# Expert gate and up weights loaded in runs of 2 KB, with the token rows stored in permuted channel order

## The chip, the cores and the metric

The program runs on one core of a Trainium2 chip. Its five engines work side by side: TensorE (PE, matrix products), VectorE (DVE), ScalarE (ACT), GpSimd (POOL) and SyncE (SP, which issues most of the transfers). Sixteen DMA engines of the core move data between DRAM and the on-chip memory of 128 partitions. The metric is the device time of one execution in microseconds, lower is better.

## The reference, cut to what matters

Two decoder layers over 1024 tokens of 1024 channels. Each layer has four mixers side by side, an output projection, and then a mixture of experts. The last part is what the change touches:

```python
def hier_moe(h, w_rg, b_rg, w_re, b_re, w_gate, w_up, w_down):
    ...
    for e in range(N_EXPERTS):
        he = jax.nn.silu(t @ w_gate[e]) * (t @ w_up[e])
        y = y + comb[:, e:e + 1] * (he @ w_down[e]).astype(f32)
    return y.reshape(B, S, D).astype(h.dtype)
...
x = x + hier_moe(rms_norm(x, ffn_norm[l]), ...)
```

There are 16 experts per layer. `w_gate[e]` and `w_up[e]` are [1024, 256], `w_down[e]` is [256, 1024], all in float32. Each token goes to two experts; `comb` is zero for the others.

## The kernel before

**Mixing stage.** `mix_stream` takes the eight token tiles of 128 tokens in order. `mix_b` multiplies a tile by the output projection, adds the residual (xm), writes it to the accumulator in DRAM (L1505; `xacc` in layer 0, the output in layer 1), and computes the second norm: L1509 is one VectorE instruction over [128 tokens, 1024 channels] that multiplies xm by the inverse root r1 and by the gain, and L1510 writes the result to `hbuf` in DRAM, one row of 4 KB per token. `mix_c` computes the routing logits from xm, not from the normed tile. The stage is interleaved with the last attention tiles.

**Expert stage.** `moe` walks 16 experts. The first two are fixed; the other 14 come by falling token count, a wide tile (256 slots) and a narrow one (128 slots) in turn. For expert e the program's order is: `expert_up(e)`; `expert_in(e+1)`; the weights W(e+1), with their loads and conversions; the gather G(e+2); `expert_down(e)`. The kernel is written against a framework that plans the order in which instructions stand on each engine, allocates the rotating buffers and puts in the waits, so the order on an engine need not be that of the text.

- `gather` (L1799): an indirect transfer, issued by POOL, fetches 128 rows of `hbuf` by slot number into xg; one per narrow expert, two per wide one.
- `expert_in`: PE transposes xg (eight blocks of 128 channels), ACT and DVE write the transposed tile as a rounded part and a remainder, xh[:, k] and xl[:, k], k = 0 to 7. Partition p of block k holds channel 128 k + p of the row as it is stored.
- `expert_weights` (L1741 to L1755): four units u of gate and up, two of down. A unit is a raw tile of [128, 1024] float32 (4 KB per partition). For gate and up, unit u holds the two channel blocks k = 2u and 2u + 1 of both matrices, laid out as (k, t, n): block, matrix (0 gate, 1 up), 256 columns. Each matrix comes with one transfer of 256 KB (L1749), in which each partition has two pieces, rows 256 u + p and 256 u + 128 + p, of 1 KB each. The raw tiles rotate through six places, one expert's worth, so that a load can start when the conversion of the same unit of the expert before is done.
- `split_unit`: each unit is converted in two halves of 512 columns, on ACT (rounded part wh, L165) and on DVE (remainder wl, L173). With the layout (k, t, n) a half is one block k of both matrices.
- `up_wide`, `up_narrow`: products over k and t, three matmuls for each (wh with xh, wh with xl, wl with xh, in either operand order), L177 to L179.
- `expert_down` (L1867): ACT scales the product rows (L1866), and POOL issues an indirect transfer that adds 128 rows of 4 KB to the accumulator in DRAM. Since all of them write the same tensor, they follow one another.

SP issues all loads and plain stores, POOL all gathers and scatter-adds. In the profile, queue q1 carries SP's transfers and q0 POOL's; both run on the same 16 DMA engines.

Of the kernel before, what the change touches and what calls it, by code (L numbers as in the profile page):

```python
# [14 lines left out]
ALU = mybir.AluOpType  # L15
# [3 lines left out]
D = 1024  # L19
# [23 lines left out]
class Region:  # L43
    """Tiles laid out by hand in pages of 8 KB: per page its kind (r: only float32r, f: anything else) and a list of
    (tag, 4-byte columns, copies). A tag with a plus shares its place with the tag after it; a tag may have copies in
    several pages. A page is taken when its first tile is, so that a phase can start while the one before it still
    holds other pages."""
# [35 lines left out]
def both(*gens):  # L83
    """alternates between generators; returns their results"""
    res = [None] * len(gens)
    live = list(range(len(gens)))
    while live:
        for k in list(live):
            try:
                next(gens[k])  # L90
            except StopIteration as e:
                res[k] = e.value
                live.remove(k)
            else:
                yield
    return res


class Trunk:
# [14 lines left out]
    # ---------------------------------------------------------------- tiles  # L114
# [23 lines left out]
    def psum(self, two):  # L138
        """the other four banks: two pairs (two) or four single ones"""
        if self.pq:  # L140
            self.pq[0].close()
        c = ExitStack()
        self.pqn += 1
        self.pq = (c, c.enter_context(self.tc.tile_pool(name=f"pq{self.pqn}", bufs=1, space=PSUM, reuse_waits="tile")), two)
# [9 lines left out]
    # ---------------------------------------------------------------- helpers  # L154
# [3 lines left out]
    def copy(self, out, in_):  # L158
        """a copy on ScalarE, every third on VectorE"""
# [31 lines left out]
    def rsqrt(self, ms, k):  # L191
        """(ms + eps) ** -0.5 for a [P, k] tile of mean squares"""
# [19 lines left out]
    # ---------------------------------------------------------------- constants  # L212
    def constants(self):
# [11 lines left out]
        # -1 on the real half, +1 on the imaginary half  # L225
# [7 lines left out]
    # masks, block scores, routing  # L233
    def constants2(self):
# [19 lines left out]
        # block scores that are forced or lie ahead: [128 q, tile, 16]  # L254
# [11 lines left out]
        # routing: token order, slots, small counters  # L266
# [20 lines left out]
    # reduced sine and cosine of an angle tile, each in [-pi, pi]  # L287
# [21 lines left out]
    # cos and signed sin tables: [128 tok, tile, half pairs], mla 16 pairs then nsa 8 pairs  # L309
# [27 lines left out]
    def rope(self, x, B, half, i, e1, e2):  # L337
        """x [P, B, 2 * half] in place, with row i of the tables, on two engines"""
# [13 lines left out]
    # ---------------------------------------------------------------- layer vectors  # L352
    def layer_vectors(self, l):
# [14 lines left out]
        # queries carry the scale of the scores and a minus  # L368
# [7 lines left out]
        # [128 ch, 2 chunks, ...]  # L376
# [14 lines left out]
        # softplus(-lam) = max(-lam, 0) + log1p(exp(-|lam|)), log1p(e) = 2 atanh(e / (2 + e))  # L391
# [24 lines left out]
        # block-diagonal gate weights [128 in, (gate, chunk), 128 out]  # L416
# [12 lines left out]
    # ---------------------------------------------------------------- input projection  # L429
    def mixer_norm(self, l, src):  # L430
        """pre-norm and its transposed halves hT"""
# [25 lines left out]
    def mixer_in(self, l):  # L457
        """channel-major columns of w_in: yields (first column, half of the tokens, psum)"""
# [14 lines left out]
    def tok_units(self, l, part, V):  # L473
        """token-major columns: c_q c_kv k_pe gate (part 0) or nsa_q k_slc v_slc k_win v_win (part 1)"""
# [18 lines left out]
    def mixer_in_tok(self, us):  # L493
        """yields (token tile, its columns), and None after each quarter of the products"""
# [20 lines left out]
    def mla_weights(self, l, V, pages):  # L515
        """up-projections, split, in the free columns 728.. of the pages, 256 columns at a time"""
# [22 lines left out]
    def prep_nsa(self, l, i, z, V):  # L539
        """queries, keys and values of a token tile, normalised and rotated, to zq"""  # L540
# [18 lines left out]
    def prep_mla(self, l, i, z, V):  # L559
        """queries, keys and values of a token tile, normalised and rotated, to zm; gates to zq"""  # L560
# [47 lines left out]
    # ---------------------------------------------------------------- RG-LRU  # L608
# [47 lines left out]
    # ---------------------------------------------------------------- S5  # L656
    # Chunks of 8 steps: y = K u + C A^(t+1) s, s' = A^8 s + sum A^(7-t) B u, with s kept in a frame that
    # turns with the phase of A^8, so that the recurrence over chunks is real.
    def s5_gen(self, l, wide):
        """tables of a layer; wide: mostly on the vector engine, phases of eight groups at once in raw pages"""  # L660
# [67 lines left out]
        # the sign of the imaginary phases, per half  # L728
# [25 lines left out]
        # input matrix times (A - 1) / a  # L754
# [42 lines left out]
        # powers in falling order  # L797
# [4 lines left out]
        for b in range(4):  # L802
# [27 lines left out]
            # response to a step, lags 7 .. 0, then zeros  # L830
# [20 lines left out]
    # u, psum [128 ch, 512 tok] -> ud [256 ch, 8, 128]  # L851
# [19 lines left out]
    def s5_block(self, l, b, io):  # L871
        """four groups, in three steps"""
# [27 lines left out]
        # rows (t, c'): column s' of row t holds lag 7 - s' - t  # L900
# [25 lines left out]
    def s5_run(self, l):  # L926
        """all blocks, staggered"""
# [47 lines left out]
    # ---------------------------------------------------------------- NSA  # L975
    def nsa_compress_in(self, half, pt):
        """k_cmp | v_cmp channels; each with a copy shifted by one token below or above it"""
# [10 lines left out]
    def nsa_compress(self, l, V):  # L988
        nc, v, I = self.nc, self.nc.vector, self.I
        hid = []  # L990
        for nm, src, o in (("k", self.KC, 0), ("v", self.VC, 1)):
# [5 lines left out]
            # token 16 c + 2 j (+ parity on the second half of the partitions)  # L997
# [57 lines left out]
    def nsa_prep(self, i):  # L1055
        """transposed and split queries and keys of tile i, its compressed blocks and its block choice"""
# [43 lines left out]
    def nsa_cmp(self, q):  # L1100
# [12 lines left out]
        # rows without a block keep their sum at zero  # L1113
# [54 lines left out]
    def merge_out(self, po, heads, P):  # L1168
        """transposed output rows [P, heads * 128], P = 64 channels or 128, their two halves [Vh | Vl]"""
# [4 lines left out]
    def merge(self, ot, y, heads, coef, first, tag, P):  # L1174
        """y [128, heads, 64] (+)= coef [128, heads] * output rows"""
# [14 lines left out]
    def soft(self, S_, k, n, P, acc):  # L1190
        """P = exp(min(S_) - S_) and its row sums, for k rows of n negated scores"""
# [7 lines left out]
    def nsa_scores(self, q, br):  # L1199
        """probabilities of the selected blocks (br 0) or of the window (br 1); two heads at a time where they are short"""  # L1200
# [70 lines left out]
    def nsa_stream(self, tiles):  # L1271
        """the token tiles in order, each next to the preparation of the one after it"""
# [16 lines left out]
    def beside(self, run, side, i):  # L1289
        """steps of run, each with one of the side generator, whose result goes to Qn[i]"""  # L1290
# [102 lines left out]
    def mla_stream(self):  # L1393
        """pairs of token tiles in order, the scores of a head next to the values of the one before"""
# [15 lines left out]
    # ---------------------------------------------------------------- output projection, router  # L1410
    def mix_stream(self, l, src):
        """w_out with the residual, the second norm and the routing logits, pipelined over the token tiles"""
# [29 lines left out]
    def out_weights(self, l):  # L1442
        """w_out times the gains of its inputs, split"""
# [13 lines left out]
    def mix_a(self, i):  # L1457
        """mixer outputs of a token tile, normalised, transposed and split"""
# [17 lines left out]
    def mix_b(self, i, yT):  # L1476
        """projection and residual, then the second norm"""
# [18 lines left out]
        else:  # L1496
            # both halves together, so that the pages of w_out come free early
# [11 lines left out]
        v.scalar_tensor_tensor(xt, xm, r1, mx["fgain"], op0=ALU.mult, op1=ALU.mult)  # L1509
# [3 lines left out]
    def mix_c(self, i, h, r1):  # L1513
        """routing logits"""
# [581 lines left out]
```

## Time and profile before

| | |
|---|---|
| device time, median of 3 runs | 2251.12 us |
| lowest and highest run | 2242.23 and 2265.75 us |
| span of the profiled execution, first to last instruction | 2249.8 us |
| bytes moved by DMA | 301.49 MB in 268,176 packets |
| packets of queue q1 (SP) | 253,592 with 246.82 MB |
| packets of queue q0 (POOL) | 14,400 with 52.44 MB |
| engines' share of the span | PE 84%, DVE 59%, ACT 49%, POOL 27% |

The profile is of one execution, and gives the span alone, not that execution's device time. An engine's busy time is the sum of its instructions; a share over the whole span is a mean over stages with different limits, so the stages are read by windows of time. "Idle before" an instruction is put down to what came last by the profile. A DMA packet is one contiguous run that one DMA engine moves.

### The profile page before, as it was taken

What the parts mean: (1) busy time and instruction counts of PE and PEld (TensorE: products, weight loads), DVE (VectorE), ACT (ScalarE), POOL (GpSimd) and SP (SyncE); (2) the same over time, 40 slices, a digit from 0 to 9 for tenths busy, and PEclk for the clock granted to TensorE, in tenths of its full rate; (3) what the DMA queues carried; (4) which work ended last, traced back from release to release, by engine and by line L of the source; (5) the groups of instructions that cost most, each with busy time, mean ns of one, the idle gap of its engine ahead of it and who ended that gap; (6) DMA issues with size and microseconds to landing.
All of it is one profiled execution on the core that took longest, in us unless ns stands there. A gap on an engine that the chain in (4) does not pass through costs nothing. (4 is left out here: it accounts for less than half of the span.)

```text
span 2249.8 us, 32167 instructions
## 1 busy us (share of the span) xinstructions
PE 1896.9 (84%) x10722; PEld 1491.7 (66%) x10722; DVE 1324.1 (59%) x3167; ACT 1112.7 (49%) x2432; POOL 616.0 (27%) x1007
## 2 busy tenths in 40 slices
PE   4759899999899877867767798999999998788886
PEld 3548876656677766756656578765557776777775
DVE  5966655465565567865534356555665555766663
ACT  4055544455454435544544555445654453465553
POOL 2432542000111136666411215420101111322121
PEclk9879998899999878988988899988998998899998
DMA  7345332022212548867774353320222124598874
GB/s 191 127 109 134 112 119 67 24 57 86 77 62 83 191 122 230 236 203 229 205 185 151 99 125 114 116 68 24 62 91 67 68 88 180 164 267 241 257 215 113
DMA packets 268176, 301.49 MB, mean 134 GB/s; under 512 B 93784, under 2 KB 221656, under 8 KB 267992
## 3 DMA queue, kind: packets, MB, share of 16 engines
q1 hardware_dynamic: 253592, 246.82, 34.9%
q0 software_dynamic: 14400, 52.44, 10.5%
q8 instruction: 89, 1.46, 0.3%
q14 instruction: 95, 0.78, 0.1%
HBM read 215.79 MB, written 78.18 MB: 131 GB/s over the span
## 5 line engine op out<-in xcount | busy, mean ns | idle before, releaser
L173 DVE TENSOR_TENSOR wl<-raw,wh 128x512 fp32r<-128x512 f32 (+3 forms) x294 | 221.1, 778 | 94.6 <-ACT wh L165 87.7
L165 ACT ACTIVATE wh<-raw 128x512 fp32r<-128x512 f32 (+3 forms) x294 | 182.5, 658 | 132.7 <-PE ps L178 54.5
L177 PE MATMUL ps<-mo,wh 128*128 128x256 f32 x576 | 169.5, 296 | 19.1 <-ACT mo L165 19.0
L1195 DVE TENSOR_REDUCE mx<-ps 128x1 f32<-128x640 f32 (+11 forms) x160 | 133.1, 832 | 77.8 <-PE ps L1229 53.1
L178 PE MATMUL ps<-mo,wh 128*128 128x256 f32 x576 | 167.5, 292 | 0.0
L179 PE MATMUL ps<-mo,wl 128*128 128x256 f32 x576 | 165.6, 289 | 0.0
L165 ACT ACTIVATE mo<-ptt 128x512 fp32r<-128x512 f32 x132 | 77.3, 597 | 138.0 <-PE ptt L210 137.7
L173 DVE TENSOR_TENSOR mo<-ptt,mo 128x512 fp32r<-128x512 f32 x132 | 90.2, 686 | 89.7 <-ACT mo L165 89.3
L210 PE MATMUL ptt<-ident,xg 128*128 128x128 f32 x400 | 69.3, 315 | 80.7 <-DMA xg<-hbuf,mo 80.0
L177 PEld LDWEIGHTS ps<-mo,wh 128*128 128x128 f32 x576 | 113.9, 198 | 23.1 <-ACT mo L165 23.1
L1197 ACT ACTIVATE P<-ps,mx 128x640 f32<-128x640 f32 (+7 forms) x128 | 89.0, 698 | 59.5 <-DVE mx L1195 50.4
L210 PEld LDWEIGHTS ptt<-ident,xg 128*128 128x128 f32 x400 | 55.5, 163 | 90.4 <-issue 69.1
L178 PEld LDWEIGHTS ps<-mo,wh 128*128 128x128 f32 x576 | 113.6, 197 | 0.1
L179 PEld LDWEIGHTS ps<-mo,wl 128*128 128x128 f32 x576 | 113.5, 197 | 0.1
L1185 POOL TENSOR_TENSOR at<-at,mt 128x256 f32<-128x256 f32 x32 | 25.2, 787 | 316.7 <-DVE mt L1181 156.6
L177 PE MATMUL ptx<-wh,mo 128*128 128x512 f32 x240 | 101.6, 423 | 3.4 <-ACT ch L1141 1.7
L198 POOL TENSOR_TENSOR rr<-rv,mhalf 128x1 f32<-128x1 f32 (+5 forms) x98 | 101.3, 1034 | 7.8
L173 DVE TENSOR_TENSOR wl<-mo,wh 128x512 fp32r<-128x512 f32 x128 | 94.8, 767 | 13.5 <-ACT wh L165 11.9
L177 PE MATMUL ps<-wh,hT 128*128 128x364 f32 (+1 forms) x256 | 97.2, 380 | 0.0
L179 PE MATMUL ptx<-wh,mo 128*128 128x512 f32 x240 | 96.8, 403 | 0.0
L1799 POOL DMA_INDIRECT xg<-hbuf,mo x50 | 53.9, 1078 | 152.1 <-PE pto L179 67.2
L178 PE MATMUL ptx<-wl,mo 128*128 128x512 f32 x240 | 95.5, 398 | 0.0
(634 smaller groups left out, 5773.9 us busy)
## 6 DMA issues: line engine op xcount, KB each, us to landing
raw<-in_moe_w_gate_dram SPq DMA_DIRECT2D x96, 256.0 KB
raw<-in_moe_w_up_dram SPq DMA_DIRECT2D x96, 256.0 KB
mo<-in_moe_w_down_dram SPq DMA_DIRECT2D x32, 512.0 KB
raw<-in_moe_w_down_dram SPq DMA_DIRECT2D x32, 512.0 KB
zm<-mqk SPq DMA_DIRECT2D x16, 512.0 KB
wo<-in_w_out_dram SPq DMA_DIRECT2D x16, 512.0 KB
mo<-yd SPq DMA_DIRECT2D x16, 512.0 KB
hbuf<-xr SPq DMA_DIRECT2D x16, 512.0 KB
```

Source lines behind the costliest of these rows:

```text
L165: self.nc.scalar.activation(out, in_, AF.Copy)
L173: e.tensor_tensor(out, in_, hi.bitcast(F32), op=ALU.subtract)
L177: mm(out, lh, rh, start=start, stop=False)
L178: mm(out, lh, rl, start=False, stop=False)
L179: mm(out, ll, rh, start=False, stop=stop)
L198: g.tensor_tensor(r, v, self.mhalf[:P, 0:1].to_broadcast([P, k]), op=ALU.pow)
L210: self.nc.tensor.transpose(out, in_, self.ident[:k, :k])
L1185: g_.tensor_tensor(y, y, a, op=ALU.add)
L1195: v.tensor_reduce(mx, S3, axis=AX.X, op=ALU.min)
L1197: nc.scalar.activation(P[j][:, 0:n], S3[:, j], AF.Exp, bias=mx[:, j:j + 1], scale=-1.0, accum_out=acc[:, j:j + 1])
L1799: self.nc.gpsimd.indirect_dma_start(out=xg, out_offset=None, in_=self.hbuf[l], in_offset=bass.IndirectOffsetOnAxis(ap=ix, axis=0))
```

## The change

Channels of the normed rows are stored in another order: position 128 k + p of a row of `hbuf` now holds channel 8 p + k. Block k of a transposed tile so has channel 8 p + k on partition p, and the rows of the gate and up matrices that partition p needs for all eight blocks, 8 p to 8 p + 7, are neighbours in DRAM. A unit takes two of them, 2 KB per matrix and partition, still with one transfer of 256 KB per matrix and unit. The raw tile is laid out as (t, k, n), so that a half of it in `split_unit` is one matrix with both blocks; the products take their operands at the new offsets. In L1509 both inputs are read in the permuted order, with a step of 8 floats in the innermost dimension, and written in sequence. The down matrices, the routing and the spill path's structure stay. Comments were also dropped in many places.

```diff
@@ mix_b
-        v.scalar_tensor_tensor(xt, xm, r1, mx["fgain"], op0=ALU.mult, op1=ALU.mult)
+        perm = lambda t: t.rearrange("q (p k) -> q k p", k=8)
+        v.scalar_tensor_tensor(xt.rearrange("q (k p) -> q k p", k=8), perm(xm), r1, perm(mx["fgain"]),
+                               op0=ALU.mult, op1=ALU.mult)
         nc.sync.dma_start(mx["hbuf"][rows, :], xt)
@@ expert_weights
-            rv = r.rearrange("p (k t n) -> p k t n", k=2, t=2)
+            rv = r.rearrange("p (t k n) -> p t k n", k=2, t=2)
             for t, nm in enumerate(("moe_w_gate", "moe_w_up")):
-                nc.sync.dma_start(rv[:, :, t], src(nm, 256 * u, 256, slice(0, 256)).rearrange("(k p) n -> p k n", p=128))
+                w = src(nm, 0, D, slice(0, 256)).rearrange("(p k) n -> p k n", k=8)
+                nc.sync.dma_start(rv[:, t], w[:, 2 * u:2 * u + 2])
@@ up_wide
-                    o = 512 * (k % 2) + 256 * t + 128 * c
+                    o = 512 * t + 256 * (k % 2) + 128 * c
@@ up_narrow
-                o = 512 * (k % 2)
-                wh, wl = [u[:, o:o + 512].rearrange("p (t n) -> p t n", t=2)[:, :, cs] for u in gu[k // 2]]
+                wh, wl = [u.rearrange("p (t k n) -> p t k n", t=2, k=2)[:, :, k % 2, cs] for u in gu[k // 2]]
```

## Rows read from the trace of the kernel before

**Rows 1.** The page: the span.

```profile
span 2249.8 us, 32167 instructions
```

**Rows 2.** Windows, expert stage of layer 1: us, engines' busy (x), PEclk, DMA share, GB/s.

```profile
2030.00:2070.00 40.00, 33.33 (x234) 29.76 (x233) 25.72 (x65) 22.90 (x46) 8.28 (x7) 0.91 0.82 243
```

**Rows 3.** Waits of PE (us, times, longest): 800 to 1180, then 1925 to 2250.

```profile
PE ptt L210 <- DMA xg<-hbuf,mo: 36.7, 5, 15.1
...
PE ptt L210 <- DMA xg<-hbuf,mo: 30.7, 7, 6.4
```

**Rows 4.** Timeline of POOL: start, us, line, operation [idle before <- releaser].

```profile
2169.95 1.00 POOL L1799 DMA_INDIRECT xg<-hbuf,mo  x1 [0.30 <-DVE wl L173]
2184.05 0.97 POOL L1799 DMA_INDIRECT xg<-hbuf,mo  x1 [13.11 <-PE pto L179]
...
2186.57 1.60 POOL L1867 DMA_INDIRECT out_dram<-mo,mo  x1 [0.30 <-issue]
2195.81 1.73 POOL L1867 DMA_INDIRECT out_dram<-mo,mo  x1 [7.63 <-ACT mo L165]
2206.83 1.64 POOL L1867 DMA_INDIRECT out_dram<-mo,mo  x1 [9.29 <-ACT wh L165]
2208.78 0.99 POOL L1799 DMA_INDIRECT xg<-hbuf,mo  x1 [0.31 <-PE ps L179]
```

**Rows 5.** Line L1867 (scatter-add), 1940 to 2240 us: time from issue to landing.

```profile
DMA to landing us min/median/max: 5.9/9.1/10.3
```

**Rows 6.** Line L1799 (gather), 1940 to 2240 us: time from issue to landing.

```profile
DMA to landing us min/median/max: 5.4/6.8/8.3
```

**Rows 7.** Timeline of PE: it takes gathered tokens, narrow expert, then wide.

```profile
2178.20 0.41 PE L210 MATMUL ptt<-ident,xg 128*128 128x128 f32 x2 [4.65 <-DMA xg<-hbuf,mo]
...
2194.50 0.60 PE L210 MATMUL ptt<-ident,xg 128*128 128x128 f32 x4
```

**Rows 8.** DMA, 2030 to 2070 us: busy tenths of 40 slices; queue's packets, MB, share.

```profile
DMA  8899999999999999999926999999981000009468
...
q1 hardware_dynamic: 4928, 6.29, 46.0%
```

**Rows 9.** DMA, 2195 to 2196.5 us, gate and up loads alone.

```profile
DMA packets 595, 0.57 MB, mean 383 GB/s; under 512 B 34, under 2 KB 595, under 8 KB 595
```

**Rows 10.** DMA, 93 to 95 us, stores with runs of 2 KB.

```profile
DMA packets 425, 0.77 MB, mean 386 GB/s; under 512 B 48, under 2 KB 48, under 8 KB 425
```

**Rows 11.** DMA, 1899 to 1901 us, loads of w_down with runs of 4 KB.

```profile
DMA packets 242, 0.83 MB, mean 416 GB/s; under 512 B 26, under 2 KB 43, under 8 KB 242
```

**Rows 12.** Timeline of SP, two loads of L946, then DMA, 1372.5 to 1376.2 us.

```profile
1371.49 0.90 SPq L946 DMA_DIRECT2D raw<-vd  x2
...
DMA packets 661, 0.54 MB, mean 146 GB/s; under 512 B 405, under 2 KB 405, under 8 KB 661
```

**Rows 13.** Waits of ACT: 800 to 1180, then 1925 to 2250.

```profile
ACT wh L165 <- DMA raw<-in_moe_w_up_dram: 12.1, 3, 7.7
...
ACT wh L165 <- DMA raw<-in_moe_w_up_dram: 8.9, 6, 4.0
```

**Rows 14.** Lines of DVE by form: line, operation, shapes xcount | busy us, mean ns.

```profile
L173 DVE TENSOR_TENSOR mo<-ptt,mo 128x512 fp32r<-128x512 f32 x132 | 90.2, 686 | 89.7 <-ACT mo L165 89.3
...
L1509 DVE SCALAR_TENSOR_TENSOR xr<-xm,rr,mo 128x1024 f32<-128x1024 f32 x16 | 21.5, 1342 | 20.2 <-POOL rr L198 17.0 <-ACT P L1197 1.9 <-DMA out_dram<-xm 1.3
```

**Rows 15.** Line L999: duration ns min/median/max, first and last start, form.

```profile
L999 DVE TENSOR_TENSOR cxk<-KC,pek x2: 1011/1022/1033, 209.6 to 1336.6; 128x504 f32<-128x504 f32 x2
```

**Rows 16.** Windows, mixing stage of layer 0, columns as in rows 2.

```profile
640.00:680.00 40.00, 39.78 (x214) 29.58 (x214) 20.38 (x30) 18.77 (x41) 6.21 (x9) 1.00 0.19 70
```

**Rows 17.** Waits of PE, 600 to 785 us, the longest for DVE.

```profile
PE ptt L210 <- DVE mo L1470: 1.1, 2, 0.7
```

**Rows 18.** Timeline of DVE and POOL at the end of layer 1's mixing.

```profile
1904.17 0.24 DVE L1528 SCALAR_TENSOR_TENSOR mo<-ptx,rr,mo 128x20 f32<-128x20 f32 x1 [1.98 <-PE ptx L1527]
...
1915.55 1.14 POOL L1799 DMA_INDIRECT xg<-hbuf,mo  x1 [2.77 <-DVE mo L1791]
```

## The prediction

> **What bounds the kernel now.** I read the page first, then TensorE's waits, then POOL's queue, then the DMA queues. The span is 2249.8 us [rows 1]. The gate and up loads of L1749 belong to the expert stage, at 800 to 1180 us in layer 0 and 1925 to 2250 us in layer 1 (loads for the first expert come a little earlier), so only what this stage waits for can be won. There PE is busy 33 us of 40, and the DMA engines 82% of the time [rows 2]: neither is full. PE's longest wait is for gathered tokens, 36.7 us in layer 0 and 30.7 us in layer 1 [rows 3]. No product waits there for wh or wl, the converted weights.
>
> Why are gathers late? POOL's queue tells [rows 4]. Gathers (L1799) and scatter-adds (L1867) take turns in it, and a scatter-add follows the one before only when that has landed: 2186.57 to 2195.81 is 9.24 us, beside a median landing of 9.1 us [rows 5]. From the gather of one narrow expert (2169.95) to that of the next (2208.78) are 38.83 us, one pair of experts. That is the loop to shorten: 8.25 us until PE has the tokens at 2178.20 [rows 7], 5.85 us of PE up to the wide expert's gathers at 2184.05, 2.52 us of POOL, scatters of 9.24 and 11.02 us, and 1.95 us of POOL. Together 38.83. Some 28.5 of it is landing time of POOL's own transfers.
>
> **What the loads do to that loop.** A scatter lands in 5.9 us at best and 9.1 in the median [rows 5], the gather here in 8.25 against 5.4 at best [rows 6]. The surplus is 2 x 3.2 + 2.85 = 9.25 us per pair: what the shared engines cost, mostly to weight loads, which move 6.29 MB per 40 us on q1 [rows 8]. Two experts' gate and up matrices are 4 x 1024 x 256 x 4 bytes = 4.19 MB of this, 67%. So at most 0.67 x 9.25 = 6.2 us per pair hang on these loads, and they shrink only as the loads do.
>
> **Runs of 2 KB for 1 KB.** In a stretch with gate and up loads alone, 1 KB runs move at 383 GB/s [rows 9]; 4 KB runs of another load at 416 [rows 11]. The nearest stretch with 2 KB runs that keeps the engines busy has 386, but it stores [rows 10]. So 4.19 MB take 10.95 us now, and 10.86 (386) to 10.08 (416) after: the saving lies between 0.09 and 0.87 us a pair. A line through the 1 KB and 4 KB rates, per run and engine (16 x 1024 / 383 = 42.8 ns, 16 x 4096 / 416 = 157.5 ns), gives 81 ns for 2 KB, 405 GB/s, 10.36 us and a saving of 0.59. Being nearest in size, the store speaks for less; I take 0.35 us, 3.2% of the load time. On the loop that is 0.032 x 6.2 = 0.20 us a pair (bounds 0.05 and 0.49), and with 16 pairs in both layers **-3 us** (-0.8 to -7.9). If all of the saved DMA time were path, it would be 16 x 0.87 = 14 us.
>
> The 1 KB rate stands 8% below the 4 KB one. [...]
>
> **That the runs really merge.** The new source has a partition's two rows as neighbours in two dimensions (k, n). L946 has such a source too; two of these 256 KB loads pass in a stretch with 661 - 405 = 256 packets of 2 KB or more [rows 12], 128 per load, one 2 KB run per partition. So I expect 128 packets of 2 KB per load and 32,768 fewer packets in all (256 loads x 128).
>
> **Halves by matrix instead of by k.** A half of the raw tile held both matrices, so each conversion waited for both loads; now the first needs gate alone. No wait is added. ACT waits for the up load 12.1 us (3 times) in layer 0 and 8.9 us (6) in layer 1 [rows 13]; were gate always there long before, 21.0 us of ACT time would go. But up is issued right behind gate on one queue, and ACT is busy only 23 us in 40 [rows 2], with its evictions alone on the loop: **-1 us** (0 to -21). In return PE needs both halves of a unit before its first pair of products; since no product waits for wh or wl now, that is nothing, and without this lead at most one half's conversion per expert, 32 x 0.69 = 22 us [rows 14].
>
> **The permuted norm (L1509).** 16 instructions of 1.34 us [rows 14] now read both inputs at a step of 8 floats. No row has two strided inputs. One, at a step of 16: 1.02 us for 504 elements [rows 15] against 0.69 us for 512 [rows 14], some +0.67 ns per element. For 1024 elements and one to two such inputs that is +0.69 to +1.37 us, in all 11 to 22 us of DVE; were a step of 8 free, zero. I take the top, 22 us, for the engine, as both inputs are strided, but nearly nothing for the time: in this stage PE is busy 39.8 us of 40 and DVE 20.4 [rows 16], and PE's longest sum of waits for DVE is 1.1 us [rows 17]. For the last tile, where the router follows, the next DVE instruction comes after 1.98 us of idling at 1904.17, and the rows of hbuf are wanted by the first gather, at 1915.55 [rows 18]. So **+1 us** (0 to 22 without this cover).
>
> The matmul operands of L1824 and L1842 only change offsets; counts and shapes stay. SP issues as many DMAs; fewer runs may save it a few hundredths each, and it bounds nothing. Sum: -3 - 1 + 1 = **-3 us**. The span of 2249.8 us is 1.3 us below the median of the runs, 2251.1, so I put the change on the median: **2248 us**. About 1% (22.5 us) is what a measurement of this kernel can tell from no change; the three runs themselves spread over 23 us.
>
> **Rivals.**
> 1. *The whole saving lands.* POOL's loop gives back every saved DMA microsecond: 2251 - 14 = 2237. For it: the engines are full in most slices of a pair's time; against it: in others they stand still [rows 8], 82% in all. Chance 0.07.
> 2. *Larger turns hurt POOL's transfers; slower.* Queue q0 shares the engines with q1. If the two alternate packet by packet, each q0 packet of a scatter waits for 81 ns, not 43. With 128 rows on 16 engines that is 8 x 38 = 0.30 us per transfer; three on the loop, 16 pairs: +15 us, 2266. It decides when loads are in flight through all three transfers and their earlier end gives nothing back. Against it: what a larger turn moves is gone from the backlog. Chance 0.08. [...]
> 3. *The planner lays the queues differently.* The order is not the program's: line 1896 comes before 1897, yet the narrow gather stands behind a scatter (2206.83, 2208.78) and the wide one's before (2184.05, 2186.57) [rows 4]. The planner works from its own durations and from waits, and the change alters both. (a) Narrow gathers move ahead of the scatter: PE's waits of 30.7 + 36.7 = 67 us could go. PE's own 33 us per 40 then bounds the loop, and not every gather will move; 40%, 27 us, gives 2224. Chance 0.20. (b) Wide gathers slip behind a scatter: the first lands at about 2184.05 + 6.8 = 2190.9 [rows 4, 6], PE takes it at 2194.50 [rows 7], a lead of 3.6 us; issued 9.24 us later, PE would wait 5.6 us a pair, and in a third of the 14 pairs with a narrow expert that is 26 us, 2277. Chance 0.12.
> 4. *No gain from 2 KB, or no merging:* 2251. Chance 0.05.
>
> **How the numbers follow.** The forecast has the remaining 0.48, with a range of its own of 2238 to 2262 from the bounds above and half the spread of the runs. Faster by over 1% (below 2228.6) needs 3a: 0.20. Slower by over 1% (above 2273.6) needs 3b or a tail of rival 2 or the norm uncovered: 0.14. Within 1%: 0.66. Range for 8 in 10: 2222 to 2272, which leaves the far sides of 3a and 3b out.
>
> **What the next profile should show.** 32,768 fewer packets; 2 KB runs at 390 to 410 GB/s in a stretch of pure gate and up loads; L1509's successor at 2.0 to 2.8 us with PE's busy share in the mixing stage unchanged; scatter landings in layer 1 at 8.7 to 9.1 us; the loop at 38 to 39 us. I am wrong if 2 KB runs move no faster or packets do not fall (rival 4), if landings grow by 0.3 us (rival 2), or if the scatters and gathers stand in another order on POOL (rival 3).

## The result and the profile after

The changed kernel takes 2288.1 us in the median of its runs, beside 2256.0 us for the kernel before on the same chip: ratio 1.0144, 95% interval 1.0103 to 1.0184. It is slower by more than the 1% that a measurement can tell, and outside the predicted range. The profiled execution is the shortest of the four and 19.8 us longer than that of [rows 1]. Of e2 and e7 below, slower executions than most were profiled, so of their profiles only the durations of DMA packets are used. The page after (span, DMA, queues: packets, MB, share of the 16 engines):

```profile
span 2269.6 us, 32152 instructions
...
DMA packets 235407, 301.48 MB, mean 133 GB/s; under 512 B 93784, under 2 KB 156120, under 8 KB 235224
...
q1 hardware_dynamic: 220824, 246.82, 35.6%
q0 software_dynamic: 14400, 52.44, 10.0%
```

The runs did merge: 268,176 - 235,407 = 32,769 packets fewer. But q1 held the DMA engines for 35.6% of a longer span, where it was 34.9%: as many bytes, fewer packets, and more time. Two stretches with gate and up loads alone show how that goes together, 1977.5 to 1979 us and 823.5 to 825 us (to be read against [rows 9]):

```profile
DMA packets 326, 0.61 MB, mean 410 GB/s; under 512 B 33, under 2 KB 33, under 8 KB 326
q1 hardware_dynamic: 326, 0.61, 106.4%
...
DMA packets 139, 0.26 MB, mean 172 GB/s; under 512 B 13, under 2 KB 13, under 8 KB 139
q1 hardware_dynamic: 139, 0.26, 93.0%
```

(A packet counts whole where it starts, so a short stretch can show over 100%.) At their best 2 KB runs move faster than the 383 GB/s of 1 KB runs. In the second stretch the engines are nearly as full and move less than half. From the trace's record of each gate and up packet between layer 1's first gather and last scatter-add: before, the mean is 49.0 ns and the median 46, so 2 KB take 98 ns; after, the mean is 105.1 and the median 84, with 1 in 20 above 219 ns (before, 1 in 20 above 60).

What POOL's transfers see of it (L1870, the scatter-adds, and L1803, the gathers, are lines 1867 and 1799 of before; 1950 to 2260 us; [rows 5]), PE's wait for tokens (1935 to 2280 us; [rows 3]) and a pair of experts on POOL ([rows 4]):

```profile
DMA to landing us min/median/max: 5.9/9.9/11.6
...
PE ptt L210 <- DMA xg<-hbuf,mo: 45.5, 7, 7.8
...
2188.86 0.99 POOL L1803 DMA_INDIRECT xg<-hbuf,mo  x1 [0.31 <-issue]
2204.58 0.97 POOL L1803 DMA_INDIRECT xg<-hbuf,mo  x1 [14.73 <-PE pto L179]
...
2229.34 1.00 POOL L1803 DMA_INDIRECT xg<-hbuf,mo  x1 [0.30 <-issue]
```

From narrow gather to narrow gather are 40.48 us here, where it was 38.83. Over the five such pairs of layer 1 in each trace the mean went from 39.11 to 40.54 us, and the time from a narrow gather's issue to PE taking it from 8.17 to 9.34. Over all gathers, wide and narrow, the median landing stays (6.7 us, [rows 6] has 6.8) and the longest grows from 8.3 to 9.6. The order of gathers and scatter-adds on POOL is the same. The five pairs as windows, before and after, columns as in [rows 2]:

```profile
2013.21:2208.78 195.57, 162.88 (x1152) 146.29 (x1152) 125.13 (x312) 112.25 (x221) 39.45 (x31) 0.92 0.82 235
...
2026.63:2229.34 202.71, 159.54 (x1148) 143.82 (x1147) 124.95 (x312) 111.45 (x220) 39.91 (x30) 0.92 0.78 227
```

The length less PE's busy time is PE's idle time: 6.54 us a pair before, 8.63 after.

The norm (L1511 here, all 16), and what PE waits for from DVE in layer 0's mixing stage (560 to 800 us), after and then before:

```profile
L1511 DVE SCALAR_TENSOR_TENSOR xr<-xm,rr,mo 128x1024 f32<-128x1024 f32 x16 | 37.0, 2315 | 20.2 <-POOL rr L198 16.9 <-ACT P L1197 1.9 <-DMA out_dram<-xm 1.3
...
PE pto L1260 <- DVE ntl L173: 3.3, 5, 1.2
PE ptt L210 <- DVE mo L1470: 2.8, 3, 1.5
PE ptx L1530 <- DVE xm L1504: 2.1, 1, 2.1
PE ptt L210 <- DVE mo L173: 1.7, 2, 1.2
```

```profile
PE pto L1260 <- DVE ntl L173: 1.9, 6, 0.5
PE ptt L210 <- DVE mo L1470: 1.1, 2, 0.7
PE ptx L1527 <- DVE xm L1504: 1.1, 1, 1.1
...
PE ptt L210 <- DVE mo L173: 0.2, 1, 0.2
```

9.9 us of waiting where it was 4.3. The length of a stage alone does not tell the price, because it moves with the granted clock of TensorE too: from the first norm of a layer to its last, kernels that keep L1509 take 171.2 us where the mean clock was 0.99 of the full one (e3 below, layer 0) and 177.2 where it was 0.94 (e14, layer 1). PE's idle time in that stretch moves little. Layers 0 and 1, before and then after:

```profile
606.93:778.23 171.30, 163.95 (x866) 124.39 (x864) 89.94 (x150) 82.46 (x188) 22.38 (x36) 0.99 0.31 111
1725.59:1900.92 175.33, 168.63 (x866) 128.97 (x864) 90.03 (x147) 82.56 (x187) 22.81 (x36) 0.96 0.30 107
```

```profile
599.13:777.57 178.44, 165.34 (x867) 125.32 (x864) 96.71 (x150) 82.89 (x188) 24.31 (x36) 0.98 0.31 103
1732.09:1910.84 178.75, 165.63 (x867) 125.44 (x864) 96.61 (x147) 82.61 (x187) 25.03 (x36) 0.98 0.30 103
```

PE idles 7.4 and 6.7 us before and 13.1 in both layers after; the other kernels below that keep L1509 have 6.5 to 7.6. From the first gather of a layer to its last scatter-add its idle time goes from 88.6 to 91.1 us in layer 0 and from 49.7 to 62.8 in layer 1. These four parts give 5.7 + 6.4 + 2.5 + 13.1 = 27.7 us. The span grew by less, since ahead of the first norm, where the change touches nothing, the profiled execution was 7.8 us shorter, at a mean clock of 0.92 where it was 0.90.

### The profile page after: what moved, and what is told of

Same layout as the page of the kernel before. It is cut to its first block, busy times and chain, and to the rows that moved or that the text cites. A ratio compares the mean times of both kernels' runs of the same rounds, so it can differ in the third digit from the quotient of the medians.

```text
span 2269.6 us, 32152 instructions
## 1 busy us (share of the span) xinstructions
PE 1892.6 (83%) x10722; PEld 1489.0 (66%) x10722; DVE 1339.0 (59%) x3167; ACT 1112.1 (49%) x2432; POOL 619.1 (27%) x1007
## 2 busy tenths in 40 slices
DMA packets 235407, 301.48 MB, mean 133 GB/s; under 512 B 93784, under 2 KB 156120, under 8 KB 235224
## 3 DMA queue, kind: packets, MB, share of 16 engines
q1 hardware_dynamic: 220824, 246.82, 35.6%
## 5 line engine op out<-in xcount | busy, mean ns | idle before, releaser
L177 PEld LDWEIGHTS ps<-mo,wh 128*128 128x128 f32 x576 | 113.9, 198 | 20.4 <-ACT mo L165 20.3
L1803 POOL DMA_INDIRECT xg<-hbuf,mo x50 | 53.1, 1063 | 156.5 <-PE pto L179 70.1
```

The lines of the kernel that those rows point to most:

```text
L177: mm(out, lh, rh, start=start, stop=False)
L1803: self.nc.gpsimd.indirect_dma_start(out=xg, out_offset=None, in_=self.hbuf[l], in_offset=bass.IndirectOffsetOnAxis(ap=ix, axis=0))
```

## The experiments

Two theories stood at the start. N: the norm's extra DVE time lies on the path. L: it is covered, and the loads cost everything. For the loads there were again two: T, rival 2 (larger turns of q1 hold up POOL's transfers), and P, the place that the runs are read from. For in the change a partition's 2 KB no longer come out of one block of 256 KB: neighbouring partitions read 2 KB at every 8 KB. The prediction did not look at that. Where a kernel below keeps L1509 as before while the loads are permuted, or the reverse, its expectation says so. Edits are shown abridged.

Executions of one kernel differ with TensorE's mean granted clock, which is on record for each. Over the 122 executions of the kernel before that the ratios of e1 to e16 rest on, with clocks of 0.89 to 0.91 of the full one, a straight line gives 16.5 us less for each 0.01 of clock and leaves a spread of 4 us. "At like clock" below is the difference of mean times to the kernel before on the same chip with this line taken off, and twice its standard error: an estimate from these times and clocks.

**e1, the norm alone.** L1509 as in the change, nothing else.

> The norm of L1509 alone: it writes the rows of hbuf in permuted order, and the loads stay as before (so the experts multiply permuted rows with unpermuted weights; nothing else is changed, all shapes and counts are those of before). Theory N, the norm's extra time lies on the path: an instruction grows from 1.34 to about 2.3 us, and the mixing stage of each layer, eight tiles, grows by 8 x 0.97 = 7.8 us, so 15.5 us in all, ratio 1.007; the expert stages (first gather to last scatter-add) keep their 372 and 319 us. Theory L, only the loads cost time and the norm is covered as predicted: +1 us, ratio 1.000.

Measured: ratio 1.0075 (1.0044 to 1.0107); 2.32 us an instruction. Timeline of DVE and PE around one tile of layer 0 in e1, then in before:

```profile
683.78 2.24 DVE L1509 SCALAR_TENSOR_TENSOR xr<-xm,rr,mo 128x1024 f32<-128x1024 f32 x1 [1.32 <-POOL rr L198]
685.92 0.71 DVE L173 TENSOR_TENSOR ntl<-ptt,at 128x512 fp32r<-128x512 f32 x1
...
686.68 0.50 PE L1260 MATMUL pto<-ntl,at 128*128 128x512 f32 x1 [1.07 <-DVE ntl L173]
```

```profile
672.43 1.28 DVE L1509 SCALAR_TENSOR_TENSOR xr<-xm,rr,mo 128x1024 f32<-128x1024 f32 x1 [1.33 <-POOL rr L198]
673.63 0.68 DVE L173 TENSOR_TENSOR ntl<-ptt,at 128x512 fp32r<-128x512 f32 x1
...
674.37 0.50 PE L1260 MATMUL pto<-ntl,at 128*128 128x512 f32 x1
```

Behind the norm on DVE's queue stands a remainder that PE wants next. Before, PE got it just in time and showed no wait; with 0.96 us more ahead of it, PE waits 1.07 us. In the 6 us behind five of layer 0's eight norms PE idles 0.7 to 1.0 us longer than before, behind the last 0.5; behind the second nothing is lost, and behind the seventh only later. From first to last norm, layers 0 and 1 of e1:

```profile
613.07:795.50 182.43, 170.03 (x868) 130.08 (x866) 96.98 (x149) 83.05 (x188) 24.36 (x36) 0.95 0.29 103
1748.46:1928.51 180.05, 166.71 (x868) 125.99 (x866) 96.70 (x147) 82.61 (x187) 24.93 (x36) 0.98 0.29 104
```

PE's idle time is 12.4 and 13.3 us, 11.7 more than before in all. At like clock e1 is 15 ± 3 us slower, against 15.5 expected. The stretches are 15.8 us longer than before, but that this equals the 15.5 is in part the lower clock of layer 0 (0.95, where it was 0.99). Theory L falls.

**e2, the loads alone.**

```diff
-rv[:, :, t] <- src(nm, 256 * u, 256, ...).rearrange("(k p) n -> p k n", p=128)
+rv[:, t] <- src(nm, 0, D, ...).rearrange("(p k) n -> p k n", k=8)[:, 2 * u:2 * u + 2]
```

> The change without its norm: loads in runs of 2 KB, halves by matrix and the new operand offsets, but L1509 as before (so the experts multiply unpermuted rows with permuted weights). Theory N: only the expert stages grow, to about 379 and 330 us, some 16.6 us in all, ratio 1.007; the mixing stages are as before. Theory L: nearly the whole loss of 32 us, ratio 1.014. In both the 2 KB packets of the expert stages keep their mean of about 105 ns and the scatter-adds land in 9.9 to 10.3 us in the median.

Measured: ratio 1.0059 (1.0031 to 1.0087), at like clock +15 ± 3 us; a mean packet of 103.6 ns. 1.0075 x 1.0059 = 1.0134: the two parts make up the 1.0144 of the change.

**e3, runs of 2 KB out of one block; e4, runs of 1 KB at the change's places.**

```diff
+e3: rv[:, t] <- src(nm, 256 * u, 256, ...).rearrange("(p k) n -> p k n", k=2)
+e4: rv[:, :, t] <- src(nm, 0, D, ...).rearrange("(p k) n -> p k n", k=8)[:, 2 * u:2 * u + 2]    (rv as before)
```

> As e2_loads, but partition p of unit u takes rows 256u + 2p and 256u + 2p + 1: still runs of 2 KB, but a transfer reads one block of 256 KB without gaps, where e2_loads reads 2 KB at every 8 KB (L1509 as before, so here too rows and weights do not belong together). Theory T, the larger turns of queue q1 hold up POOL's transfers (rival 2): as e2_loads, landings of 9.9 to 10.3 us, ratio 1.007. Theory P, the gaps in the source slow the packets: the mean of a 2 KB packet falls from 105 to under 92 ns, landings return to 8.7 to 9.1 us, and the 3 us of the prediction appear, ratio 0.998 to 1.000.

> As e2_loads in the source (2 rows of 1 KB that are neighbours, at every 8 KB), but laid out on the chip as before, (k, t, n), so that a partition's two rows land 2 KB apart and a run can be 1 KB at most; halves by k, offsets and order of all engines as before (L1509 as before, rows and weights do not belong together). Theory T: packets of 1 KB with turns as before, so landings of 8.7 to 9.1 us, ratio 1.000. Theory P: the gaps slow packets of 1 KB too, from a mean of 49 to 55 ns or more, landings of 9.5 us or more, ratio 1.005 or more.

| | ratio | at like clock | mean packet | gather taken by PE | pair, layer 1 | of it PE idle | scatter landing, median |
|---|---|---|---|---|---|---|---|
| before | 1 | 0 | 49.0 ns (1 KB) | 8.17 us | 39.11 us | 6.54 us | 9.1 us |
| e3 | 1.0026 (0.9999 to 1.0053) | +3 ± 3 us | 92.4 ns (2 KB) | 8.39 us | 39.19 us | 7.09 us | 8.8 us |
| e4 | 1.0064 (1.0034 to 1.0094) | +14 ± 2 us | 53.8 ns (1 KB) | 9.15 us | 40.74 us | 8.18 us | 8.9 us |
| changed kernel | 1.0144 (1.0103 to 1.0184) | | 105.1 ns (2 KB) | 9.34 us | 40.54 us | 8.63 us | 9.9 us |

Time, gather and pair follow the place of the runs, not their length. e4's packets are of 1 KB as before and its instructions stand in the order of before, yet it has the whole price of e2. Kernels whose gate and up loads are all there and as before in place and length (e1, e6, e8, e11, e12, e13, e16) have gathers of 7.6 to 8.6 us, pairs of 37.8 to 39.3 and 5.7 to 7.1 us of PE idle in a pair. So theory T does not carry the loss; theory P does. Two of P's signs failed: the 3 us that it promised for e3 did not appear, and e4's scatter-adds landed in 8.9 us, T's number, where P wanted 9.5. The median of landings does not tell these kernels apart; with loads as before it is 7.7 to 9.1. In layer 0 the last five pairs hardly see the place (46.70 us before, 46.43 in e4, 47.46 in the changed kernel).

**e7 and e9, other pitches.**

```diff
+e7: src(nm, 512 * (u // 2), 512, ...).rearrange("(p k) n -> p k n", k=4)[:, 2 * (u % 2):2 * (u % 2) + 2]
+e9: src(nm, 2 * u, 896, ...).rearrange("(p k) n -> p k n", k=7)[:, 0:2]
```

> As e2_loads, but with 2 KB at every 4 KB instead of every 8 KB: units 2h and 2h+1 share a block of 512 rows, partition p takes two of its rows 512h + 4p to 512h + 4p + 3 (L1509 as before, so rows and weights do not belong together). If the price of the gaps grows with the pitch: a mean packet between 91 and 104 ns, say 97, narrow gathers taken by PE 8.9 us after issue, ratio 1.004. If 4 KB is as good as none: 91 ns, 8.4 us, ratio 1.003 or less, as e3. If any gap costs the same: 104 ns, 9.4 us, ratio 1.006, as e2.

> As e2_loads, but with 2 KB at every 7 KB: partition p of unit u takes rows 7p + 2u and 7p + 2u + 1 (so some rows of the matrices are read twice and others not at all; as many bytes and transfers as before, L1509 as before). If a wide gap in the source is what costs: as e2, a mean packet of about 104 ns, narrow gathers taken by PE 9.4 us after issue, ratio 1.006. If it is the pitch of 8 KB itself, at which all streams stand at the same place of a repeating pattern of addresses: 91 to 94 ns, 8.4 us, ratio 1.003 or less.

Measured: e7 1.0040 (1.0009 to 1.0071), at like clock +6 ± 3 us, 93.2 ns; e9 1.0038 (0.9999 to 1.0077), at like clock +5 ± 3 us, 91.9 ns, gathers at 8.89 us (8.4 expected), a pair of 39.42 with 6.92 us of PE idle. At 7 KB the packets are as short as without gaps (91.9 ns, 92.4 in e3), at 4 KB nearly (93.2). So at these two pitches a gap costs the packets nothing to speak of; at 8 KB it does (103.6 in e2). By packets that is clear (92 and 93 against 105 ns); by the ratios e9 can't be told from e2, at like clock it can (5 against 15 us). Neither e7 nor e9 can be told from e3. Why 8 KB, no run shows; nor does one show the repeating pattern of addresses that e9's expectation names.

**e5, the permutation moved to PE.** Loads of e3; the norm as before; PE's transposes take every second channel.

> The loads of e3_runs_2k_in_one_block, and rows and weights belong together again: hbuf keeps the old order and L1509 is as before, while PE's transposes of a gathered tile (L210, ptt<-ident,xg) take every second channel of a block of 256, by a step of 2 floats in the operand. Theory F, a step in PE's operand costs nothing: as e3, ratio 1.000 to 1.003, the groups of four transposes at 0.60 us. Theory C, PE pays for the step: the groups grow to about 1.2 us and, 12 groups of four per pair of experts in either layer at 0.3 to 0.6 us, 16 pairs, partly on the loop's path: ratio 1.010 or more.

Measured: ratio 1.0026 (0.9991 to 1.0062), at like clock +3 ± 3 us. All transposes of gathered tiles, before and e5 (busy us, mean ns):

```profile
L210 PE MATMUL ptt<-ident,xg 128*128 128x128 f32 x400 | 69.3, 315 | 80.7 <-DMA xg<-hbuf,mo 80.0 <-DVE mo L173 0.6
```

```profile
L210 PE MATMUL ptt<-ident,xg 128*128 128x128 f32 x400 | 75.6, 333 | 88.8 <-DMA xg<-hbuf,mo 87.5 <-DVE mo L173 1.2
```

The mean moves within one kernel too (before: 291 ns from 1960 to 2060 us, at a mean clock of 0.96, and 331 from 2060 to 2160, at 0.90). Over a whole execution it is 326 to 333 ns with the step (e14, e15, e5), and 313 to 322 without it in the kernels with all loads whose profiles are used here. So a step of 2 floats costs PE some 10 ns a transpose, an estimate from these ranges, and against e3, which has the same ratio, nothing in the time. Theory F holds.

**e6, e13, e16: halves by matrix.** e6 and e16 are one kernel, the layout (t, k, n) with runs of 1 KB; e13 converts it by k.

```diff
-a half: r[:, 512 * k:512 * k + 512]
+e13: r.rearrange("p (t k n) -> p t k n", t=2, k=2)[:, :, k]
```

> Only the layout (t, k, n) on the chip: halves by matrix and the new operand offsets, with the old rows, old channels and the norm as before; loads stay in runs of 1 KB without gaps. It brings the order of instructions that the change has. Theory O, this layout with its order costs what e3 had left over: ratio 1.003 and a pair's loop in layer 1 as e3's, 39.2 us. Theory M, it costs nothing or gives the 1 us of the prediction: ratio 0.999 to 1.001.

> The layout (t, k, n) of e6 with the old rows and runs of 1 KB, but each half converted by block k of both matrices, as before the change (operands of two pieces of 256 columns). Theory H, halves by matrix, with the order on ACT and DVE that they bring, cost the 0.2 to 0.3% that e3, e5 and e6 had left over: ratio 1.000. Theory A, it is the layout or the offsets of the products: ratio 1.002 to 1.003, as e6.

> e6 once more, beside e13 on the same chip: by theory H 1.002 to 1.003 and above e13; if e6 was chance, 1.000 and as e13.

Measured: e6 1.0022 (0.9986 to 1.0058), e13 0.9999 (0.9966 to 1.0032), e16 0.9980 (0.9950 to 1.0009); at like clock +1, -2 and -1 us, each ± 3 to 4. The surplus of e6 did not come back: this step of the change is worth nothing that can be measured, either way.

**e10, half of the gate and up loads.** The up matrices are left out.

> Before, but the up matrices are not loaded: the conversions read each gate block twice (the step of the copied operand is 0), so that engines, products, gathers and scatter-adds do the same work and q1 moves 4.19 instead of 6.29 MB per pair of experts. The prediction's step (a) says that at most 6.2 us of a pair's loop hang on the gate and up loads; half of them gone would give up to 3.1 us a pair, a loop of 36 us in layer 1 and, over 16 pairs, up to -50 us: ratio 0.978 to 0.99. Rival: the loop hardly hangs on the volume of the loads, and what they take from POOL's transfers is set by the few packets ahead of them: a loop of 38.5 us or more, ratio 0.995 to 1.000.

Measured: ratio 0.9838 (0.9790 to 0.9885). A pair takes 35.47 us, a narrow gather 6.83. The five pairs, landings of scatter-adds (1940 to 2215 us) and PE's wait for tokens (1925 to 2250 us):

```profile
2009.07:2186.41 177.34, 158.84 (x1160) 142.76 (x1159) 124.72 (x312) 111.63 (x221) 40.51 (x31) 0.96 0.77 205
...
DMA to landing us min/median/max: 6.2/7.2/10.6
...
PE ptt L210 <- DMA xg<-hbuf,mo: 17.6, 7, 3.9
```

The loop does hang on these loads. PE's idle time falls from 6.54 to 3.70 us a pair, 2.84 less; the other 0.8 us of the 3.64 by which a pair is shorter go with a clock of 0.96, where it was 0.92. From the first gather of layer 1 on, loads for 14 experts pass, seven pairs; their packets took 87.9 us of the 16 engines before and 45.2 now, 6.1 us a pair less. So each of these gives back 0.60 us of the pair, 0.47 of it PE's waiting. Layer 0 gains less: its last five pairs go from 46.70 to 45.29 us, with 1.40 us less of idle time each. For the whole kernel, at like clock, e10 is 21 ± 5 us faster than before.

**e14, the change without norm, pitch and halves by matrix.** Loads and transposes of e5, halves as in e13.

> The change without its three costs: runs of 2 KB in one block of 256 KB as in e5 (PE permutes, the norm as before), and halves by k as in e13. In e3 the gate and up packets took 82.8 us of the engines in layer 1 against 87.9 before, 0.64 us a pair; e10 took 5.3 us a pair away and gained 3.64. If the loop gives back the same share here: 0.44 us a pair, 16 pairs, -7 us, ratio 0.997. If a small saving is lost in where the transfers fall: ratio 1.000.

Measured: ratio 1.0011 (0.9986 to 1.0037), at like clock +2 ± 3 us; a mean packet of 90.5 ns, a pair of 39.11 us. In layer 1 the gate and up packets take 81.1 us of the engines where it was 87.9, 0.97 us a pair less (the expectation had divided by eight pairs where seven are counted), and the pair is as long as before. The expected 7 us lie outside the interval; with layer 0 gaining less, as in e10, they were too many. Why nothing of the saving shows is open: narrow gathers take 8.58 us in e14 and 8.42 in e15, 8.17 before and 7.57 in e13, which would fit rival 2's 0.3 us a transfer, but e6 and e16 have 8.56 and 8.57 with runs of 1 KB.

**e8, e11, e12, e15: the norm in other forms.** e8 gives it to POOL in two steps; e11 reads only xm in steps; e12 has the inverse root alone and puts the gain into the conversions; e15 is e14 with e12.

```diff
+e8:  gpsimd.tensor_scalar(xt, xm, r1, mult); gpsimd.tensor_tensor(xt, xt, fgain, mult)
+e11: scalar_tensor_tensor(permuted xt, permuted xm, r1, fgain in sequence)
+e12: tensor_scalar(xt, xm, r1, mult)
+     split_unit: scalar.activation(h, r, Copy, scale=g[:, k]); scalar_tensor_tensor(l, r, g[:, k], h, mult, subtract)
```

> Before, but L1509's product is made by POOL in two plain steps (times the inverse root, then times the gain), nothing permuted; loads as before. Theory N, what stands behind the norm on DVE sets PE's pace in 7 of 8 tiles: DVE is rid of 1.34 us a tile, so 2 x 7 x 1.0 to 1.3 us go, against which the last tile of each layer reaches hbuf some 3 us later: -8 to -15 us, ratio 0.993 to 0.997. Theory Q, the queue only passes the delay on: POOL's two steps (some 4 us) hold up the roots of the next tile and products of the attention, and the ratio is 1.000 or above.

> e1_norm with one strided input instead of two: xm is read at a step of 8 floats, the gain in sequence (so the gains belong to other channels, and rows and weights do not belong together; loads as before). An instruction should take about 1.8 us (1.34 + half of 0.97). Theory N, each microsecond of DVE here is one of the path: half the price of e1, ratio 1.0035 to 1.004. Rival: there is a cover of about half a microsecond which the two inputs used up: ratio 1.000 to 1.001.

> Before, but L1509 multiplies by the inverse root alone (one input), and the gain goes into the conversions of gate and up, as a scale per partition on ACT and a two-step remainder on DVE; the loads are as before. By the nearest rows, 0.42 and 0.64 us for 512 elements, the norm would take 0.8 to 1.2 us, so theory N gives 14 x 0.15 to 0.5 us: -2 to -7 us, ratio 0.997 to 0.999. Rival: the scaled conversions (0.04 us more for each half on ACT by the rows of 1024 elements, 1.14 against 1.05 us) stand on the expert stage's path and take it back: ratio 1.000 to 1.002.

> e14 with the gain in the conversions as in e12 (the scales taken in the permuted order, the norm with one input): if the two add up, 0.995 times the ratio of e14, 0.992 to 0.995. If conversions of two pieces with a scale are slower, or the order of instructions turns against it: 0.996 or more.

The norm's rows in e8 (two), e11 and e12:

```profile
L1509 POOL TENSOR_SCALAR xr<-xm,rr 128x1024 f32<-128x1024 f32 x16 | 47.9, 2997 | 1.7
L1509 POOL TENSOR_TENSOR xr<-xr,mo 128x1024 f32<-128x1024 f32 x16 | 38.8, 2425 | 1.2
```

```profile
L1509 DVE SCALAR_TENSOR_TENSOR xr<-xm,rr,mo 128x1024 f32<-128x1024 f32 x16 | 36.2, 2261 | 20.2 <-POOL rr L198 19.2 <-ACT P L1197 1.0
```

```profile
L1509 DVE TENSOR_SCALAR xr<-xm,rr 128x1024 f32<-128x1024 f32 x16 | 13.0, 811 | 20.2 <-POOL rr L198 17.9 <-DMA out_dram<-xm 1.3 <-ACT P L1197 1.0
```

| | ratio | at like clock | norm | PE idle from first to last norm, layers 0 and 1 |
|---|---|---|---|---|
| e8 | 1.0194 (1.0150 to 1.0238) | +31 ± 4 us | 5.4 us on POOL | 18.4 and 18.7 us |
| e1 | 1.0075 (1.0044 to 1.0107) | +15 ± 3 us | 2.32 us on DVE | 12.4 and 13.3 us |
| e11 | 1.0055 (1.0018 to 1.0091) | +12 ± 3 us | 2.26 us on DVE | 11.4 and 12.8 us |
| before | 1 | 0 | 1.34 us on DVE | 7.4 and 6.7 us |
| e12 | 0.9949 (0.9914 to 0.9984) | -3 ± 3 us | 0.81 us on DVE | 6.3 and 5.9 us |
| e15 | 0.9975 (0.9945 to 1.0006) | +1 ± 3 us | as e12 | 6.5 and 6.5 us |

The longer norm on DVE costs most of its added length (in e1 11.7 us of PE's idle time for 16 x 0.98 = 15.7 us); the shorter one does not give its length back. The norm of e12 is shorter by 0.53 us, 8.5 us in 16 instructions, but PE's idle time falls by 1.9 us only, because in the 6 us behind each layer's first seven norms it idled for 0.5 us at most before. e12 is 11 us faster by its ratio (interval 4 to 19; 9 by the means), where 2 to 7 were expected; most of that goes with a higher clock, 0.9035 in the mean of its executions beside 0.9000 before, and e15 has 0.9038 beside 0.9001. Whether the kernel brings the higher clock, no run shows. Of the kernels that do the whole work e12 is the only one with an interval below 1. e11 missed its number since one strided input costs nearly as much as two; by its length it should have about e1's time, and at like clock has somewhat less (12 against 15 us). In e8 the queue only passes the delay on: DVE's wait for the next tile's roots (L1470, 560 to 830 us) is

```profile
DVE mo L1470 <- POOL rr L198: 22.4, 6, 9.1
```

against 7.9 us before. e15 does not add to e12; the intervals overlap.

## Why the prediction was wrong, by its steps

**The norm: cost right, cover wrong.** Of the engine's cost the prediction took the top, 22 us; 16 x 0.97 = 15.6 us were measured, within its bounds of 11 and 22. The step that failed is the next: "nearly nothing for the time", from PE busy 39.8 us of 40, DVE 20.4, and PE's longest wait for DVE of 1.1 us [rows 16, 17]. A wait of 1 us tells that PE's operands come in time; how early they come it doesn't tell. They came just in time behind six of layer 0's eight norms (e1): the norms' 0.97 us more each became 11.7 us more of PE's idle time in the two layers, and e1 is 1.0075 times before. DVE's idle half was no cover either, because it lies in front of the norm (9.2 us of waiting for the roots in 560 to 800 us) and between links of PE's chain. And the full PE was a sign for the path, not against it: what held it up added to the end (e1, 15 us at like clock). The prediction named the whole price without cover, 22 us, but left it among the tails of its 0.14 for slower and made it no rival of its own.

**The runs of 2 KB: the rate right, the transfer wrong.** 390 to 410 GB/s were expected and are there, in the best stretches (410 from 1977.5 us on). The term was sized from the length of the runs alone. The change also moved where they are read, and at every 8 KB the packets' mean rose by 7% (105.1 ns for 2 KB, where it was 98) instead of falling by 3%. No row that the prediction used shows such a source. Still, the source's address formula stood in the diff, and a case for "the new source is slower" should have stood among the rivals. e2 and e4 measured it at 1.0059 and 1.0064, some 13 to 14 us (at like clock 15 and 14), where the forecast had 3 us the other way.

**The loop: right in layer 1.** What was said of POOL's queue and of its dependence on the loads was borne out: e10 takes 2.84 us of PE's waiting off a pair for half of the loads, where the step had at most 3.1 (6.2 for all). It is the same loop that turned the longer packets into time. But the step was read from layer 1 and counted for the 16 pairs of both; in layer 0 the pairs gain half as much (e10), and what the changed kernel's expert stages cost lies nearly all in layer 1 (13.1 us of idle time beside 2.5). Scatter-adds' landings, which the prediction named as a sign, do not tell the kernels apart (e4).

**Merging: right** (32,768 packets expected, 32,769 measured). **Halves by matrix:** -1 us expected, nothing measurable found.

**The rivals.** 1 is out: e14 frees the engines and gains nothing. 2 had the right sign, place (gathers) and size (15 us), but not the cause: e4 has its price with packets of 1 KB, so that the size fits is luck. That the two queues alternate packet by packet, on which its 0.30 us a transfer rests, no run shows; what the runs show is a narrow gather taken after 8.39 us beside packets of 2 KB (e3) and after 9.15 us beside packets of 1 KB (e4). 3 is out as a cause: the order of POOL's transfers did not change. 4 came nearest in words, with no gain from 2 KB, but without the two losses.

## What to carry to other kernels

Before work is added to an engine that is half idle, look at what stands behind it in that engine's queue and who takes that next: "no wait" means just in time or early, and only the times of the hand-over tell which (here 0.97 us more a norm, with PE's longest wait at 1.1 us before, became 11.7 us of PE's idle time). A change of layout for longer runs has two sides, the length of a run and the pitch between runs; both are read from the source's address formula, and the packets' mean, not the best stretch, tells what they cost (here 105.1 ns, where two packets of 1 KB took 98, beside a best stretch of 410 GB/s, where it was 383). Work whose inputs needn't be permuted in the long chain is better permuted where a step is cheap (here PE's transposes, some 10 ns each, beside 0.97 us for a norm). Shortening such work is another matter: where the taker waits 0.5 us at most, no more than that can come back (here 1.9 us in all from the gain moved into the conversions). And kernels whose executions run at different clocks are compared by an engine's idle time, or at like clock, before a gain is put down to an edit.

## What the runs showed of the hardware

- Loads of 128 partitions at a pitch of 8 KB: a mean of 105.1 and 103.6 ns per packet of 2 KB (changed kernel, e2) and 53.8 per 1 KB (e4), against 92.4 (e3) and 49.0 (before) without gaps, 93.2 at 4 KB (e7) and 91.9 at 7 KB (e9). In the changed kernel the median is 84 ns, below two of the 46 before, and 1 packet in 20 is above 219, where it was 60: there the tail makes the difference.
- A VectorE product of two float32 inputs of 128 x 1024 elements took 1.34 us (before), 2.26 with one input at a step of 8 floats (e11), and 2.32 with two (e1): the price of two is nearly that of one.
- The same product in two plain steps on GpSimd took 3.00 and 2.43 us (e8), and a one-input product with a scalar per partition on VectorE 0.81 us (e12).
- The kernel before took 16.5 us less for each 0.01 of TensorE's mean granted clock (122 executions, 0.89 to 0.91 of the full clock, an estimate by a straight line); from first to last norm, PE's idle time in the kernels that keep L1509 was 6.5 to 7.6 us, at clocks from 0.94 (e14, layer 1) to 0.99 (before and e3, layer 0).
